# Two transformer blocks in one kernel: norms in two parts, and small work moved beside products

## The chip, the cores and the metric

One core of one Trainium2 chip. The time is that of one execution on the device, in microseconds (us). The kernel runs all its matrix products on TensorE (PE) with float32 data, and each product is three passes over split operands. VectorE (DVE), ScalarE (ACT) and GpSimd (POOL) prepare operands and do everything between the products; SyncE (SP) issues the loads.

## The reference

512 tokens of width 1024 go through two blocks, one after the other.

First block: `h = rms_norm(x, attn_norm)`; `proj = h @ w_in` gives queries, keys and values of a stick-breaking attention of 8 heads (sb), and the latent inputs `cq` (384 columns) and `ckv` (256, with 32 more for a rotary key) of a second attention of 8 heads (MLA) whose heads are normed and rotated by position. `x = x + concat(rms(sb), rms(mla)) @ w_o`. Then a feed-forward by product keys (PEER): `h = rms_norm(x, ffn_norm)`, keys `h @ peer_w_q`, the best 16 of 128 x 128 experts for each of 8 heads, and `x = x + sum(g * gelu(h . u[idx]) * v[idx])`.

Second block: `mod = silu(c) @ w_ada + b_ada` is cut into `sh1, sc1, g1, sh2, sc2, g2`; `hn = rms(x, norm1_g) * (1 + sc1) + sh1`; a mixer of three parts (6 Fox heads with a running sum of log gates, 4 mLSTM heads, 6 MoBA heads); `x = x + g1 * (y @ w_out)`; `hn = rms(x, norm2_g) * (1 + sc2) + sh2`; `x = x + g2 * ((silu(hn @ w_gate) * (hn @ w_up)) @ w_down)`.

## The kernel before, in words

The order of the work is written out by hand, engine by engine; nothing reorders it. Tokens lie in 4 tiles of 128 on the partitions, and the normed input of a product lies transposed as 8 chunks of 128 features by 512 tokens. Every float32 operand is kept as a high and a low part (`hhi`/`hlo`, `whi`/`wlo`), and a product of one chunk is three matmuls (L329 to L331). Weights come through one stream: a load of up to 128 x 1024, a cast to the high part on ScalarE (L198), and a subtraction for the low part (L200) on VectorE, or on GpSimd where the entry says so; two blocks are prepared ahead.

Two shapes of product: `tok_gen` (tokens on the output's partitions, weights streaming, four banks, one for each token tile) and `feat_gen` (features on the partitions, 512 tokens streaming, one bank). `beside` runs a second generator of small steps in step with a product, one step after each group of three matmuls; `mix` does so with a budget of time.

The norms (`Norm`, L382) take the token tiles in a given order. Three tiles have their sums early, the last one late, since the product before ends with it. `late` scales three tiles, transposes them for four chunks (L423), scales the last tile when its own reciprocal root is there (L431), then goes on chunk by chunk: transpose the last tile into the same bank (L436), and `norm_out` over all 512 columns (L444). With a shift, `norm_out` is a scaled and shifted copy, a cast, and a subtraction; without, a scaled cast and one fused subtraction. The product that follows starts after that.

Where the small work stands: the trigonometric tables of the rotary embedding come after the products `cq` and `ckv` on VectorE (L670 to L705), ahead of the roots that norm these (`latent_T`). The heads of MLA are normed and rotated beside products (`head_norm_gen`, L736), then transposed (`head_T`, L768). The sb queries and keys for head pairs 0 to 3 are products of `feat_gen`; pairs 0, 1 and 2 stand beside the head norms, pair 3 beside the first attention (L857). The PEER expert tiles `u` (128 experts each, 384 of the 512 tokens) are made in three places: 40 early ones during the scores and the building of the gate matrix, the rest in the big loop over 128 key rows. The Fox queries and keys are normed beside the next product (`fox_q`, `fox_k`, L1440 to L1460), and the side generator goes on at once from the norm to its transposes (L1421). The modulation (`ada_gen`) runs on GpSimd, one block after each weight block that is fetched. The rows `g1`, `g2` are spread over all partitions by eight small products with a diagonal matrix (`row_from_cols`, L1332), each by itself, ahead of what needs them.

```python
def beside(main, side):
    for ns in main:
        yield ns
        r = next(side, None)
```

## Time and profile before

| | us |
|---|---|
| median of 3 runs | 2392.91 (2389.0 to 2395.34) |
| the profiled execution's own time | 2386.05 |
| its span | 2384.3 |
| TensorE busy | 2272.4 (95%) |
| VectorE busy | 1603.8 (67%) |
| GpSimd busy | 1085.2 (46%) |
| ScalarE busy | 967.2 (41%) |
| mean granted TensorE clock | 0.971 of 2.4 GHz |

The busy time of TensorE counts a matmul at either clock level; the slices of the page with a granted clock of 8 tenths are those in which part of the time ran at 1.2 GHz. Idle time of the other engines costs nothing by itself.

### The profile page before, as it was taken

The page shows a single profiled execution, that of the slowest core. Times are in us where ns is not written, and L with a number is a line of the kernel's source. Part 1 is how long each engine was busy: PE and PEld are TensorE (multiplying, and loading weights), DVE is VectorE, ACT ScalarE, POOL GpSimd, SP SyncE. Part 2 cuts the span into 40 slices and gives each one's busy share as a digit, 9 for nine tenths or more (in the row PEclk, how much of TensorE's full clock was granted, in tenths as well). Part 3 has the DMA queues.
Part 4 walks back from the last instruction along what each step waited for, and adds up shares of the span by engine and source line. Part 5 has one row for each costly group of instructions (what it writes and reads, how often), then busy time and mean ns, then how long its engine had stood idle before and what let it go on. Part 6 is the DMA issues. An engine that isn't in the chain of part 4 may idle for free.

```text
span 2384.3 us, 31909 instructions
## 1 busy us (share of the span) xinstructions
PE 2272.4 (95%) x11721; PEld 1948.5 (82%) x11721; DVE 1603.8 (67%) x2979; ACT 967.2 (41%) x1712; POOL 1085.2 (46%) x763
## 2 busy tenths in 40 slices
PE   7899999988989999999999999999799998999999
PEld 7777778878878888888888888888797776888787
DVE  5666639999967788888888877875675355433322
ACT  4556633446763333333333333335454434222211
POOL 4460024645766666776667666643656102500000
PEclk9998999999999999999999999999899899999999
DMA  5430042325688888998989888962342112423231
GB/s 169 137 115 1 11 154 88 104 96 197 238 292 304 306 303 298 319 313 310 331 306 320 307 307 306 317 235 90 128 131 93 45 36 71 158 92 98 85 112 56
DMA packets 174936, 439.91 MB, mean 184 GB/s; under 512 B 16956, under 2 KB 71100, under 8 KB 171708
## 3 DMA queue, kind: packets, MB, share of 16 engines
q1 hardware_dynamic: 136188, 301.28, 37.6%
q0 software_dynamic: 36864, 134.23, 15.5%
q10 hardware_dynamic: 1728, 2.36, 0.3%
q8 instruction: 92, 1.51, 0.3%
q14 instruction: 64, 0.52, 0.1%
HBM read 406.10 MB, written 31.72 MB: 184 GB/s over the span
## 4 chain that ended last, share of the span: by engine, by line
PE 70%; DVE 15%; issue 5%; POOL 4%; ACT 3%; DMA 2%; SPq 0%; ACTq 0%; POOLq 0%; DVEq 0%
PE bank L331 20%; PE bank L329 20%; PE bank L330 20%; DVE ohAB L1114 3%; DVE ohA L1121 3%; PE bank L571 2%; POOL rows L1241 2%; PE bank L582 2%; POOL wlo L200 2%; PE bank L563 1%; DVE wlo L200 1%; DMA w<-in_uT_dram 1%; PE bank L811 1%; DVE eq L1054 1%; DMA w<-in_peer_v_dram 1%
## 5 line engine op out<-in xcount | busy, mean ns | idle before, releaser
L200 POOL TENSOR_TENSOR wlo<-w,whi 128x1024 fp32r<-128x1024 f32 (+2 forms) x154 | 398.4, 2590 | 416.8 <-ACT whi L198 367.9
L331 PE MATMUL bank<-hhi,wlo 128*128 128x384 f32 (+1 forms) x1600 | 576.0, 360 | 11.3 <-POOL wlo L200 10.9
L329 PE MATMUL bank<-hhi,whi 128*128 128x384 f32 (+1 forms) x1600 | 579.7, 362 | 0.7 <-ACT ge L914 0.7
L330 PE MATMUL bank<-hlo,whi 128*128 128x384 f32 (+1 forms) x1600 | 573.3, 358 | 1.4 <-DVE hlo L455 1.4
L198 ACT CAST whi<-w 128x1024 fp32r<-128x1024 f32 (+4 forms) x414 | 420.9, 1024 | 322.2 <-PE bank L331 173.8
L200 DVE TENSOR_TENSOR wlo<-w,whi 128x1024 fp32r<-128x1024 f32 (+2 forms) x260 | 326.9, 1259 | 277.3 <-ACT whi L198 275.4
L331 PEld LDWEIGHTS bank<-hhi,wlo 128*128 128x128 f32 x1600 | 303.5, 190 | 39.2 <-POOL wlo L200 16.3
L329 PEld LDWEIGHTS bank<-hhi,whi 128*128 128x128 f32 x1600 | 303.5, 190 | 34.1 <-issue 4.1
L330 PEld LDWEIGHTS bank<-hlo,whi 128*128 128x128 f32 x1600 | 303.4, 190 | 30.2 <-DVE hlo L455 2.0
L330 PE MATMUL bank<-wlo,ch 128*128 128x512 f32 x768 | 304.7, 397 | 4.5 <-DVE wlo L200 4.4
L329 PE MATMUL bank<-whi,ch 128*128 128x512 f32 x768 | 304.3, 396 | 4.3 <-DMA w<-in_uT_dram 2.8
L331 PE MATMUL bank<-whi,cl 128*128 128x512 f32 x768 | 304.4, 396 | 0.0
L1219 DVE TENSOR_TENSOR cl<-ge,ch 128x384 fp32r<-128x384 f32 x125 | 148.5, 1188 | 140.4 <-ACT ch L1218 139.5
L1241 POOL DMA_INDIRECT rows<-in_peer_v_dram,eidx x128 | 183.2, 1432 | 109.7 <-DVE acc L1264 81.8
L1241 POOL DMA_INDIRECT rows<-in_peer_u_dram,eidx x128 | 178.5, 1394 | 99.6 <-DVE junk L1259 75.3
L1259 DVE SCALAR_TENSOR_TENSOR junk<-rows,h 128x1024 bf16<-128x1024 f32 x128 | 188.3, 1471 | 0.5 <-DMA rows<-in_peer_u_dram,eidx 0.2
L1264 DVE SCALAR_TENSOR_TENSOR acc<-rows,coefg,acc 128x1024 f32<-128x1024 f32 x127 | 181.6, 1430 | 0.7 <-DMA rows<-in_peer_v_dram,eidx 0.4
L330 PEld LDWEIGHTS bank<-wlo,ch 128*128 128x128 f32 x768 | 144.8, 189 | 36.6 <-DVE wlo L200 5.3
L329 PEld LDWEIGHTS bank<-whi,ch 128*128 128x128 f32 x768 | 144.8, 188 | 36.2 <-ACT ch L1212 3.1
L331 PEld LDWEIGHTS bank<-whi,cl 128*128 128x128 f32 x768 | 144.9, 189 | 35.7 <-DVE cl L1219 0.6
L329 PE MATMUL bank<-whi,hhi 128*128 128x384 f32 (+3 forms) x448 | 170.5, 381 | 0.0
L914 ACT ACTIVATE ge<-bank 128x384 f32<-128x384 f32 x116 | 57.1, 493 | 269.8 <-PE bank L331 265.7
(384 smaller groups left out, 3553.5 us busy)
## 6 DMA issues: line engine op xcount, KB each, us to landing
w<-in_uT_dram SPq DMA_DIRECT2D x128, 512.0 KB
w<-in_peer_v_dram SPq DMA_DIRECT2D x128, 512.0 KB
ada_w<-in_w_ada_dram SPq DMA_DIRECT2D x96, 256.0 KB
gdram<-gs SPq DMA_DIRECT2D x24, 1024.0 KB
gblk<-gdram SPq DMA_DIRECT2D x16, 1536.0 KB
w<-in_w_gu_dram SPq DMA_DIRECT2D x44, 512.0 KB
w<-in_w_down_dram SPq DMA_DIRECT2D x22, 512.0 KB
w<-in_w_pq_dram SPq DMA_DIRECT2D x16, 512.0 KB
```

Of the source, the lines that this page charges most:

```text
L198: nc.scalar.copy(hi[:, :n], t[:, :n])
L200: (eng or nc.vector).tensor_tensor(lo[:, :n], t[:, :n], hi[:, :n].bitcast(F32), op=OP.subtract)
L329: nc.tensor.matmul(o, ah, bh, start=start, stop=False)
L330: nc.tensor.matmul(o, ah, bl, start=False, stop=False)
L331: nc.tensor.matmul(o, al, bh, start=False, stop=stop)
L914: nc.scalar.activation(t, b[:, :DTOK], AF.Gelu)
L1114: nc.vector.tensor_tensor(AB.rearrange("p c b i t -> p (c b) i t"), iota4, IJ[:, n].rearrange("p c (b t) -> p (c b) t", t=2).unsqueeze(2) ...
L1121: nc.vector.tensor_tensor(A[:, c], AB[:, 0], g_, op=OP.mult)
L1219: nc.vector.tensor_sub(cl, t, ch.bitcast(F32))
L1241: nc.gpsimd.indirect_dma_start(out=r, out_offset=None, in_=A["peer_" + kind], in_offset=bass.IndirectOffsetOnAxis(ap=eidx[:, k:k + 1], axi ...
L1259: nc.vector.scalar_tensor_tensor(junk, r, 1.0, h2, op0=OP.mult, op1=OP.mult, accum_out=preg[:, k:k + 1])
L1264: nc.vector.scalar_tensor_tensor(acc, r, coefg[:, k:k + 1], acc, op0=OP.mult, op1=OP.add)
```

## The change

Nine edits, all of order and grouping; what is computed is the same.

1. `Norm` no longer keeps banks for all four tiles. `late` transposes three tiles of all eight chunks and writes their 384 columns at once; the last tile is scaled after chunk 3 and is transposed and written by a generator `tail` in two halves of four chunks, at given steps of the product that follows (`with_tail`).
2. `tok_gen` has `head`: the first two weight blocks are taken tile by tile, the last tile last. It is used for `cq` and for `fvg`.
3. The tables go into a generator that runs beside `cq`.
4. The ffn norm is followed by two `u` tiles ahead of the keys' product (`HEAD`); one more `u` tile is early (`SPILL` 13, `EARLY` 41).
5. The sb products of pair 1 (queries) and pair 3 (queries) go ahead of the transposes of the MLA heads; 16 products with the tables become 4.
6. Norm 1 of the second block takes its tiles as 3, 2, 1, 0; the pools of the mixer open ahead of `late`.
7. `fox_q`, `fox_k` and `moba_heads` yield six more steps (`SLACK`) between norm and transposes; `ada_gen` multiplies with `tensor_scalar`.
8. `feat_pair` (first gate and up pair) runs over 384 columns and then over 128. The modulation beside the gated product starts after this pair and ends before the last but one.
9. The rows `g1`, `g2` are made by `row_gen`, a step at a time beside `out` block 0 and beside the last two gate products.

```diff
-NPRE = 4
+SLACK = 6
+TAIL = (4, 7)
+HEAD = 2
-U0 = 8
+U0 = 10
-SPILL = tuple(LEAD + 4 + 8 * k for k in range(12))
+SPILL = tuple(LEAD + 4 + 7 * k for k in range(13))
...
         def late(self, g):
...
-            for c in range(NPRE):
-                first(c)
-            W.ahead(2)
-            drain(g)
-            x, t, r = self._to(3)
...
+            def last():
+                drain(g)
+                x, t, r = self._to(3)
+                nc.vector.tensor_scalar(t[0], x[0], r, None, op0=OP.mult)
+                nc.scalar.mul(t[1], x[1], r)
+            for c in range(KC):
                 b = bank()
                 for i in range(3):
                     tt = self.order[i]
+                    nc.tensor.transpose(b[:, tt * P:(tt + 1) * P], self.chunk(i, c), ident)
+                sh = None if self.shift is None else self.shift[:, c:c + 1]
+                norm_out(b[:, cols], hhi[:, c, cols], hlo[:, c, cols], self.scale[:, c:c + 1], sh, self.temp, c % 2)
+                if c == 1:
+                    W.ahead(2)
+                if c == 3:
+                    last()
+                if c == 5:
+                    W.ahead(3)
+            self.tail = self.tail_gen()
+        def tail_gen(self):
+            tt = self.order[3]
+            cols = slice(tt * P, (tt + 1) * P)
+            for c0 in (0, 4):
+                b = bank()
+                for k in range(4):
+                    c = c0 + k
+                    nc.tensor.transpose(b[:, k * P:(k + 1) * P], self.chunk(3, c), ident)
+                if self.shift is None:
+                    for k in range(4):
+                        c = c0 + k
+                        norm_out(b[:, k * P:(k + 1) * P], hhi[:, c, cols], hlo[:, c, cols], self.scale[:, c:c + 1],
+                                 None, None)
+                else:
...
+                    t4 = t.rearrange("p (k n) -> p k n", k=4)
+                    nc.scalar.copy(hhi[:, c0:c0 + 4, cols], t4)
+                    nc.vector.tensor_sub(hlo[:, c0:c0 + 4, cols], t4, hhi[:, c0:c0 + 4, cols].bitcast(F32))
+                yield
...
+        if head:
+            ws = [(cp, W.get((key, cp), LOOK - n)) for n, cp in enumerate(cps[:2])]
+            b.extend(bank() for _ in range(NT))
+            for tt in head:
+                for cp, w in ws:
+                    yield from block(cp, w, tt)
...
-        for c in range(kc):
-            w_ = slice(c * P, (c + 1) * P)
-            for (wh, wl), b in zip(ws, bs):
-                mm3(b, (wh[:, w_], wl[:, w_]), (hi[:, c, :], lo[:, c, :]), c == 0, c == kc - 1)
-                yield 3 * S / 2.4
+        for t_ in (slice(0, 3 * P), slice(3 * P, S)):
+            for c in range(kc):
+                w_ = slice(c * P, (c + 1) * P)
+                for (wh, wl), b in zip(ws, bs):
+                    mm3(b[:, t_], (wh[:, w_], wl[:, w_]), (hi[:, c, t_], lo[:, c, t_]), c == 0, c == kc - 1)
+                    yield 3 * (t_.stop - t_.start) / 2.4
...
+    def with_tail(main, nx, at):
+        for k, ns in enumerate(main):
+            yield ns
+            if k + 1 in at:
+                next(nx.tail, None)
...
-                nc.gpsimd.tensor_tensor(w, w, col_, op=OP.mult)
+                nc.gpsimd.tensor_scalar(w, w, col_, None, op0=OP.mult)
...
-    proj_tok("cq", hhi, hlo, KC, 384, lambda tt, b: nc.scalar.copy(cqk[:, tt, :384], b[:, :384]))
+    drain(beside(with_tail(tok_gen("cq", hhi, hlo, KC, 384, lambda tt, b: nc.scalar.copy(cqk[:, tt, :384], b[:, :384]),
+                                   head=range(NT)), nx, TAIL), tables()))
...
         for k, x0 in enumerate((64, 80, 80, 64)):
-            for tt in range(NT):
-                nc.vector.tensor_mul(tabs[k][:, tt], s4[:, tt, :, x0:x0 + 16],
-                                     tr[:, tt, k, :][:, None, :].to_broadcast([P, NH, 16]))
-            yield 800.0
+            nc.vector.tensor_mul(tabs[k], s4[:, :, :, x0:x0 + 16],
+                                 tr[:, :, k, :].unsqueeze(2).to_broadcast([P, NT, NH, 16]))
+            yield 700.0
...
     mix(sbqk_gen(0), fill)
+    mix(sbqk_gen(1, (0,)), fill)
     fill.finish()
...
-    mix(sbqk_gen(1), fill, 0.9)
+    mix(sbqk_gen(1, (1,)), fill, 0.9)
     mix(sbqk_gen(2), fill, 0.9)
+    mix(sbqk_gen(3, (0,)), fill, 0.9)
     fill.finish()
...
+        nx = Norm(lambda tt: xs[:, tt, :], (0, 1, 2, 3), g_ffn, None, o1)
         drain(tok_gen(("o", 1), hhi, hlo, KC, 512, norm_behind(nx, o_evac(1)), O_ORDER, nx.order))
         nx.late(nx.rest)
+        for n in range(HEAD):
+            drain(with_tail(u_gen(), nx, ((6,), (2,))[n]))
...
-        nx = Norm(lambda tt: xs[:, tt, :], (3, 0, 1, 2), n1, sh1, None)
+        nx = Norm(lambda tt: xs[:, tt, :], (3, 2, 1, 0), n1, sh1, None)
...
+        nx.half = lambda: wk.tile([P, S], F32, name="nT_h", tag="f512", bufs=FB2)
+        nx.late(nx.rest)
         y = b2.tile([P, NT, D], F32, name="y")
...
-        proj_tok("fvg", hhi, hlo, KC, 398, ev_fv)
+        drain(with_tail(tok_gen("fvg", hhi, hlo, KC, 398, ev_fv, head=nx.order), nx, TAIL))
...
         def fox_q():
             yield from tq.norm()
+            for _ in range(SLACK):
+                yield
...
-            yield
+                yield
+            for _ in range(SLACK - 3):
+                yield
             yield from fox_T(tk.t, fkg, kTf)
...
-        late_["pool"], late_["g1r"] = b3, row_from_cols(g1c, b3, "g1r")
-        drain(out0)
+        late_["pool"], late_["g1r"] = b3, b3.tile([P, D], F32, name="g1r")
+        drain(beside(out0, row_gen(g1c, b3, late_["g1r"])))
...
             if f == 0:
-                drain(feat_pair((("gate", f), ("up", f)), hhi, hlo, KC, (ev_gate, ev_up)))
+                drain(with_tail(feat_pair((("gate", f), ("up", f)), hhi, hlo, KC, (ev_gate, ev_up)), nx, (8, 11)))
+                ada = ada_gen(tl, range(10, 12))
+                W.tick = ada_tick
             else:
-                proj_feat(("gate", f), hhi, hlo, KC, ev_gate)
+                if f == NF - 2:
+                    drain(ada)
+                    W.tick = None
+                    row = row_gen(g2c, b4, g2r)
+                drain(beside(feat_gen(("gate", f), hhi, hlo, KC, ev_gate), row))
```

`row_gen` makes the same eight diagonal matrices and products as `row_from_cols`, one for each step, the product of a matrix one step after the matrix.

## Rows read from the trace of the kernel before

**Rows 1.** Part 1 of the page: busy time, share of the span, instructions.

```profile
PE 2272.4 (95%) x11721; PEld 1948.5 (82%) x11721; DVE 1603.8 (67%) x2979; ACT 967.2 (41%) x1712; POOL 1085.2 (46%) x763
```

**Rows 2.** What TensorE waited for: total us, times, longest us.

```profile
PE bank L423 <- DVE rs_u L338: 21.9, 4, 11.8
PE bank L331 <- POOL wlo L200: 10.9, 9, 2.5
PE bank L1421 <- DVE cum L1449: 7.9, 1, 7.9
PE bank L375 <- DVE cqk L369: 6.8, 2, 6.3
PE bank L436 <- DVE nT_x L431: 5.8, 3, 2.1
PE bank L1421 <- DVE fx_t L1456: 4.4, 1, 4.4
PE bank L1339 <- DVE dg L1338: 4.3, 3, 2.4
PE bank L768 <- DVE m_q L760: 3.5, 1, 3.5
PE bank L436 <- DVE xb L431: 3.2, 1, 3.2
PE bank L768 <- DVE m_k L760: 1.6, 1, 1.6
```

**Rows 3.** Windows: length; busy us (count) PE, PEld, DVE, ACT, POOL; PEclk; DMA; GB/s.

```profile
21.80:38.90 17.10, 17.10 (x100) 17.10 (x99) 6.67 (x9) 6.92 (x12) 12.54 (x10) 1.00 0.44 138
70.65:75.80 5.15, 5.15 (x19) 4.36 (x20) 1.68 (x3) 1.50 (x3) 4.21 (x4) 0.51 0.29 94
222.40:239.60 17.20, 17.20 (x65) 11.95 (x63) 12.93 (x36) 10.30 (x24) 0.00 (x0) 0.50 0.00 1
327.80:340.50 12.70, 7.19 (x33) 6.49 (x33) 10.48 (x32) 6.99 (x10) 2.36 (x1) 0.65 0.34 116
510.00:690.00 180.00, 161.45 (x1346) 150.07 (x1346) 173.38 (x173) 120.72 (x280) 114.91 (x89) 0.95 0.58 205
715.00:1616.00 901.00, 894.29 (x4340) 786.43 (x4340) 724.88 (x771) 311.14 (x433) 579.84 (x339) 1.00 0.87 304
1682.50:1693.60 11.10, 3.22 (x12) 3.08 (x13) 7.82 (x12) 1.16 (x2) 8.56 (x6) 0.54 0.38 120
1712.40:1721.00 8.60, 4.21 (x20) 4.06 (x20) 4.46 (x7) 1.71 (x3) 6.53 (x6) 0.80 0.52 160
1885.00:1912.00 27.00, 25.89 (x87) 19.29 (x88) 9.45 (x31) 12.98 (x28) 5.77 (x13) 0.50 0.00 1
1947.80:1953.80 6.00, 4.25 (x18) 3.33 (x17) 3.40 (x10) 1.27 (x3) 0.00 (x0) 0.72 0.00 0
2249.80:2256.80 7.00, 4.49 (x18) 3.55 (x18) 3.43 (x10) 1.39 (x3) 0.00 (x0) 0.76 0.05 20
```

**Rows 4.** Timeline of VectorE, 52 to 71 us: start, us, instruction.

```profile
52.05 0.48 DVE L670 MEMSET chmask<- 128x512 f32 x1
...
60.18 0.22 DVE L705 TENSOR_TENSOR trig<-ang,r_k_rope_g 128x64 f32<-128x64 f32 x1
...
70.09 0.74 DVE L369 TENSOR_SCALAR cqk<-cqk,lt 128x384 f32<-128x384 f32 x2
```

**Rows 5.** Timeline of TensorE at 357.7 us: sixteen matmuls of 128 columns.

```profile
357.74 1.95 PE L993 MATMUL bank<-psc,pq 128*128 128x128 f32 x16
```

**Rows 6.** Timeline of VectorE in the last norm.

```profile
1993.28 2.20 DVE L347 TENSOR_TENSOR rs_t<-rs_t,nr_r 128x1 f32<-128x1 f32 x1
...
1995.51 0.16 DVE L349 SCALAR_TENSOR_TENSOR nr_r<-rs_t,nr_r 128x1 f32<-128x1 f32 x1
...
1998.85 0.69 DVE L455 TENSOR_TENSOR hlo<-nT_s,hhi 128x512 fp32r<-128x512 f32 x1 [0.69 <-ACT hhi L454]
...
2002.28 0.69 DVE L455 TENSOR_TENSOR hlo<-nT_s,hhi 128x512 fp32r<-128x512 f32 x1 [0.69 <-ACT hhi L454]
```

More of the change, by code (lines that the diff above doesn't have):

```diff
@@ L434, in late @@
-            for c in range(KC):
-                b = self.banks[c]
-                nc.tensor.transpose(b[:, tt * P:(tt + 1) * P], t[:, c * P:(c + 1) * P], ident)
-                sh = None if self.shift is None else self.shift[:, c:c + 1]
-                norm_out(b, hhi[:, c, :], hlo[:, c, :], self.scale[:, c:c + 1], sh, self.work, c % 2)
-                if c == 4:
-                    W.ahead(3)
-                if c + NPRE < KC:
-                    first(c + NPRE)
+                    nc.tensor.transpose(b[:, tt * P:(tt + 1) * P], self.chunk(i, c), ident)
@@ L687, in build @@
[L687 to L706 removed]
+    trig = []
@@ L1328, in build, with row_gen @@
     pst.close()
-    def row_from_cols(cols, pool, name):
-        t = pool.tile([P, D], F32, name=name)
-        for hh in range(2):
-            b = bank()
-            for k in range(4):
-                dg = pool.tile([P, P], F32, name="dg", bufs=2)
-                nc.vector.tensor_scalar(dg, ident, cols[:, hh * 4 + k:hh * 4 + k + 1], None, op0=OP.mult)
-                nc.tensor.matmul(b[:, k * P:(k + 1) * P], ones, dg, start=True, stop=True)
-            nc.scalar.copy(t[:, hh * 512:(hh + 1) * 512], b)
-        return t
-    with tc.tile_pool(name="nrm", bufs=1) as nrm:
-        nx.work = nrm
-        nx.late(nx.rest)
+    def row_gen(cols, pool, t):
+        b = dg = None
+        for k in range(9):
+            if k and k % 4 == 0:
+                nc.tensor.matmul(b[:, 384:512], ones, dg, start=True, stop=True)
+                nc.scalar.copy(t[:, (k - 4) * P:k * P], b)
+            elif k:
+                nc.tensor.matmul(b[:, (k - 1) % 4 * P:(k - 1) % 4 * P + P], ones, dg, start=True, stop=True)
+            if k == 8:
+                return
+            if k % 4 == 0:
+                b = bank()
+            dg = pool.tile([P, P], F32, name="dg", bufs=2)
+            nc.vector.tensor_scalar(dg, ident, cols[:, k:k + 1], None, op0=OP.mult)
+            yield
     with ExitStack() as st:
@@ L1462, in moba_heads @@
             yield from heads.norm()
+            for _ in range(SLACK):
+                yield
             yield from moba_T(heads.t, gain, dst)
```

216 lines of the change are left out of this document (129 added, 87 removed).

## The prediction

> **What bounds the kernel now.** The first part of the page gives TensorE 2272.4 us of work in a span of 2384.3, 95%; no other engine is above 67% [rows 1]. So a microsecond is won only where TensorE idles, where it runs at its lower clock, or where VectorE holds it for a whole stage. The view of what TensorE waited for names the idle places, and most of the large ones are one wait each [rows 2]: 11.8 us at the start and some 10.1 more over three later norms (first tiles' roots), 7.9 and 4.4 at the Fox heads, 6.3 for the normed latent, 3.5 and 1.6 for the MLA heads, 4.3 over the diagonal matrices, 3.2 and 5.8 for the norms' last tiles. The windows say what the stages are like [rows 3]: the big loop (715 to 1616) has TensorE busy 894.29 of 901.00, so work taken out there is won in full; from 510 to 690 VectorE is busy 173.38 of 180.00 and TensorE 161.45, so there VectorE sets the pace. The last thing to read in the windows is the granted clock. Behind each large wait it is about half: 0.51 from 70.65 to 75.80 behind the 6.3 us, 0.54 around the 7.9. It is also half in two attention stretches (222.4 to 239.6, 1885 to 1912) where TensorE hardly idles [rows 3]. These levels are 1.2 and 2.4 GHz, and work at the lower one takes about twice as long.
>
> **Prices used.** A matmul over 384 columns: 17.10 us over 100 = 0.171 [rows 3]; so 0.228 for 512, by the ratio. One of 128 columns: 1.95 us over 16 = 0.12 [rows 5].
>
> **Part 1, tables beside cq: -8.3.** On VectorE the tables run from 52.05 to 60.4 (8.35 us), and the step that TensorE waits for, the scaled latent, comes at 70.09 [rows 4]. All of what lies between (squares, roots) starts behind them. 8.35 earlier, that step lies ahead of the end of the values' product (the wait of 6.3 us ends at 70.65), and some 0.5 of the 6.3 us is left. With the wait goes the lower clock behind it: 5.15 us at 0.51 is about 2.5 lost. Sum -5.8 - 2.5. The cover: in cq VectorE is busy 6.67 of 17.10 [rows 3], so 8.35 fit; without that cover the tables would delay hlo and cost up to what they save. Bounds -5 (the clock stays low) and -9.
>
> **Part 2, the first norm split: -2.** The 3.2 us wait for the last tile [rows 2] goes; its eight transposes (1.0) stay, now inside cq, and I leave 0.8 for the last tile coming late behind the tables. 3.2 - 0.4 - 0.8 = 2. Bounds 0 and -4.
>
> **Part 3, MLA heads: -6.5.** Waits of 3.5 and 1.6 [rows 2]. Ahead of each now stands one more sb product, 24 matmuls x 0.228 = 5.5 us, longer than either wait. These are not new work; one leaves the first attention, where TensorE is busy in all of the window that I read. Low clock behind the 3.5, in proportion to part 1 (2.5 x 3.5 / 6.3), 1.4. The sum -3.5 - 1.6 - 1.4. That 16 small VectorE products become 4 is not in it: it only shortens a chain that is then hidden. Bounds -4 (waits for hlo of heads move) and -8.
>
> **Part 4, the ffn norm and two u tiles: +2.** Between 327.8 and 340.5 TensorE is busy 7.19 of 12.70 at clock 0.65 [rows 3]. A u tile needs the first three token tiles only: 24 x 0.171 = 4.1 us. Two of them now stand ahead of the keys' product: I put their start at 336.3 (the 24 first transposes at the low clock), so that product starts at 336.3 + 8.2 + 1.0 (tail) + 1.4 (low clock) = 347, 6.5 later than now. All that hangs on its scores is VectorE's (510 to 690), so the shift passes through. In return the big loop has one tile less: -4.1, in full. One tile less beside the gate matrix is worth only -0.5, since VectorE bounds there. +6.5 - 4.1 - 0.5 = +2. The ends: nothing is won back, +6; the shift is 1.5 only and the stretch gives 1 back, -3.
>
> **Parts 5 and 8, the two norms with a shift: +3 and -0.5.** Of `norm_out` with a shift, two chunks of 512 columns are 3.43 us apart on VectorE (1998.85 to 2002.28, rows 6). Bound for 384 columns: 3.43 x 0.75 = 2.57 and 3.43; I take 2.75, nearer the ratio. Eight chunks take 11.0, and the last tile's instructions stand behind the eighth in VectorE's order. Norm 1: the product's head has 12 groups (3 x 2 x 2) of 3 x 0.18 = 6.5 us before it needs the last tile, which comes some 2 us after the eighth chunk; TensorE waits there for about as long as it saved (one wait of the 5.8 over three), and the modulation may now start earlier, on GpSimd, during the norm: +3, between -2 and +6. Norm 2: the pair's 48 matmuls of 512 (10.9) become 48 x 0.171 + 48 x 0.12 = 14.0, +3.1, and the tail costs 1.0; against it go a wait of 2.1 for the last tile and the longest wait for a low part on GpSimd, 2.5 [rows 2], since the modulation starts after the pair: -0.5, between -4 and +4.
>
> **Part 7, the Fox heads: -12.** TensorE waits 7.9 and 4.4 [rows 2]; it has 3.22 busy at 0.54 in one window and 4.21 at 0.80 in the other, some 1.6 and 1.0 lost to the clock [rows 3]. Six steps more are 6 x 3 x 0.171 = 3.1 us later that it asks: 4.8 and 1.3 of the waits are left if VectorE's chain ends when it does now. It need not. A tiny operation that takes 0.16 takes 2.20 in another norm [rows 6], and GpSimd is busy 8.56 of the 11.10 us of the stall with the modulation [rows 3]. In the changed kernel the modulation can start earlier (the pools open before the norm, its loads with them), so less of it should be piled up here. I take half of the 6.1 as left: -9.2 - 2.6 = -12. Ends: only the shift, -6; all gone, -15.
>
> The Trainium skill ("SBUF — State Buffer", Who interferes with whom) says that a VectorE instruction with two SBUF inputs contends with a GpSimd instruction that reads SBUF, and that the one that came second waits whole. The 2.20 us agree. By that rule `tensor_scalar` on GpSimd, which still reads SBUF, takes away no block, and only how much of the modulation is left over there would count; this part would be -6 and not -12, which is the rival called port below.
>
> **Part 9, rows of g1 and g2: -3.7 and -4.3.** 1947.8 to 1953.8 and 2249.8 to 2256.8 [rows 3] hold the eight diagonal products by themselves; their 16 matmuls (two passes each) at 0.12 stay: 6.0 - 1.9 and 7.0 - 1.9, less 0.4 and 0.8 of other work in those windows. VectorE's share is hidden by the products. The ends: -2 and -4.5 for the first, -3 and -5 for the second.
>
> Sum: -8.3 - 2 - 6.5 + 2 + 3 - 0.5 - 12 - 3.7 - 4.3 = -32.3. On the profiled execution's 2386.05 this is 2353.8; the median of the runs shown lies 6.9 above that execution, so the forecast for the median is 2392.9 - 32.3 = 2361. With the parts' ends taken as independent the sum holds about 15 either way: 2346 to 2376.
>
> **The rivals.**
> *Port.* VectorE's chains stay as long as now, since GpSimd's low parts and modulation lie beside them: the Fox part gives only the -6 of its shift, norm 1 costs +6, norm 2 +4. That is +6 + 3 + 4.5 = 13.5 less won: 2374. For it speak the 2.20 us of rows 6; against it that the waits of parts 1, 3 and 9 don't hang on GpSimd.
> *Everything hidden.* The tails come in time and the modulation is out of the way: norm 1 -2, norm 2 -4, Fox -15, ffn -3: 16.5 more: 2345. VectorE's 11.0 for eight chunks speaks against it.
> *No gain: the clock.* Slower than before by one mechanism: TensorE's lower clock in the attentions. 17.2 and 27.0 us already run at half there with TensorE busy 17.20 and 25.89 [rows 3], and one dense product of 5.5 us is taken out of the first. If the lower level spreads over the stages around them, each microsecond of it costs half. To cost the 32 it needs 64 us more of the lower level; at 80 us the time is 2401. For it speaks that nothing in those two rows but the kind of work tells them from other stretches; against, that the change takes long waits away, behind which the clock falls, and leaves the attentions' own instructions as they are.
>
> **How the numbers follow.** Forecast 0.56, port 0.20, everything hidden 0.10, the clock at its full price 0.06, and 0.08 for the clock at half of it with the port (within 0.3%, about 7 us, the least that a measurement of this kernel can tell from no change). Faster 0.86, same 0.08, slower 0.06. The range goes from 2340, just beyond everything hidden, to 2384, which leaves out the two cases of no gain.
>
> **What would show it.** The wait for the latent (L369) gone or under 1 us, and full clock behind it. No wait at L768. The waits at L1421 together about 3 us; still 6 would be the port. The keys' product starting near 347. In norm 1, a wait of TensorE for hlo inside the head of fvg of about 2. The pair over gate and up 14 us long. No L1339 stretch by itself. The two windows of attention at half clock much as they are; any longer stretch of half clock there, and the prediction is wrong for the third reason.

## The result, and the profile after

The changed kernel takes 2358.15 us (median of 4 runs, 2351.38 to 2358.26); the kernel before, on the same chip, 2390.95 (2386.07 to 2395.34). The ratio is 0.9856 [0.9829, 0.9883]: faster, by 32.8 us between the medians and by 27.8 between the two profiled executions (2386.05 and 2358.26). Some executions run at a lower mean clock and take over 1.5% longer; medians and ratios leave them out. The sum of the steps was -32.3. That agrees better than its terms do, and in part by luck: parts 1, 2, 5, 8 and 9 fell short by 12.9 us together, and 8.5 came from parts 3, 4 and 7 and from stages for which nothing was forecast.

The first part of the page (busy time, share of the span, instructions), to be read beside [rows 1]:

```profile
PE 2261.8 (96%) x11769; PEld 1944.4 (83%) x11769; DVE 1586.2 (67%) x2983; ACT 971.3 (41%) x1744; POOL 1120.7 (48%) x763
```

What TensorE waited for, to be read beside [rows 2] (total us, times, longest us):

```profile
PE bank L449 <- DVE rs_u L343: 18.6, 3, 11.6
PE bank L336 <- POOL wlo L203: 10.2, 11, 2.2
...
PE bank L1435 <- DVE dg L1441: 4.3, 2, 2.5
PE bank L380 <- DVE mlo L374: 3.8, 1, 3.8
...
PE bank L334 <- ACT hhi L486: 3.4, 2, 2.7
...
PE bank L380 <- DVE cqk L374: 2.9, 2, 1.5
...
PE bank L335 <- DVE hlo L501: 1.6, 2, 1.5
PE bank L468 <- DVE nT_h L443: 1.3, 1, 1.3
```

The waits of the head transposes are gone: no line names L851 (MLA, L768 before) or L1520 (Fox, L1421 before). The waits for the diagonal matrices (`dg`) kept their 4.3 us, and the norms' last tiles are waited for under new names (`hhi` L486, `nT_h` L443).

Cut at the same products on TensorE, the two profiled executions compare by stage like this (us; each time is of one execution):

```
                                               before   after   change  forecast
start to end of the latents' two products       85.75   79.38    -6.4    -10.3  (parts 1, 2)
  of it: to the end of cq                       38.88   38.79
MLA heads, first sb products                   124.36  117.20    -7.2     -6.5  (part 3)
sb attention                                    68.35   66.43    -1.9      0
ffn norm to the PEER scores                     26.80   32.77    +6.0     +6.5  (part 4)
scores and gate matrix                         332.65  332.07    -0.6     -0.5  (part 4)
big loop, to norm 1                            937.37  930.93    -6.4     -4.1  (part 4)
norm 1 to the end of fvg                        25.89   29.69    +3.8     +3    (part 5)
end of fvg to the first Fox score               71.59   58.79   -12.8    -12    (part 7)
Fox attention                                   73.97   70.39    -3.6      0
MoBA and mLSTM                                 147.44  148.80    +1.4      0
out product with the row g1, to norm 2          44.82   42.51    -2.3     -3.7  (part 9)
norm 2 and the first pair                       22.98   27.50    +4.5     +2.0  (part 8 without its -2.5)
gated product with the row g2                  241.78  239.29    -2.5     -6.8  (part 9, and the -2.5 of part 8)
```

Part 8 counts on a wait of 2.5 for a low part that goes away. In the kernel before, that wait stands in the gated product and not in norm 2 or the pair, which end at 2014.45; so its -2.5 belongs to the last row:

```profile
2023.09 0.50 PE L331 MATMUL bank<-hhi,wlo 128*128 128x512 f32 x1 [2.52 <-POOL wlo L200]
```

The windows of the changed kernel for the main ones (length; busy us and count of PE, PEld, DVE, ACT, POOL; granted clock; DMA share; GB/s):

```profile
38.79:79.38 40.59, 37.71 (x214) 32.55 (x213) 20.00 (x41) 20.00 (x45) 28.74 (x20) 1.00 0.43 139
79.38:196.58 117.20, 117.20 (x676) 100.18 (x674) 76.43 (x202) 72.43 (x172) 60.90 (x36) 1.00 0.34 113
...
1611.24:1640.93 29.69, 24.90 (x127) 23.05 (x128) 18.33 (x38) 16.36 (x29) 14.18 (x10) 0.89 0.37 114
1640.93:1699.72 58.79, 58.79 (x367) 58.18 (x367) 30.07 (x68) 30.58 (x54) 38.07 (x26) 1.00 0.40 130
1699.72:1770.11 70.39, 68.62 (x442) 62.14 (x442) 44.18 (x142) 41.08 (x102) 56.59 (x38) 1.00 0.40 132
1770.11:1918.91 148.80, 144.32 (x665) 106.83 (x664) 70.19 (x204) 59.65 (x136) 45.30 (x51) 0.89 0.18 57
...
1961.42:1988.92 27.50, 23.43 (x129) 21.46 (x129) 15.39 (x33) 14.57 (x25) 4.74 (x2) 0.83 0.11 39
1988.92:1993.52 4.60, 4.60 (x12) 3.63 (x13) 2.42 (x3) 2.70 (x4) 1.94 (x1) 0.50 0.00 0
```

In the second and fourth of these TensorE is busy for the whole window at full clock: nothing is left to win there but work. And between the end of `fvg` and the first Fox score VectorE is busy 30.07 us for 68 instructions; the kernel before needed 40.24 for 66 (first row below). Its work became shorter, which no step of the forecast had priced.

The Fox attention is 3.6 us shorter for a plain reason: the steps move products ahead of the first score. There are 442 matmuls in it, 460 before; 18 x 0.171 = 3.1 us, and the stretch ahead of it has that much more. So the two stages are read together from here on: 145.56 before, 129.18 after, -16.4.

### The profile page after: what moved, and what is told of

The parts are those of the page before. It is cut to its first block, busy times and chain, and to the rows that moved or that the text cites. A ratio compares the mean times of both kernels' runs of the same rounds, so it can differ in the third digit from the quotient of the medians.

```text
span 2356.6 us, 32050 instructions
## 1 busy us (share of the span) xinstructions
PE 2261.8 (96%) x11769; PEld 1944.4 (83%) x11769; DVE 1586.2 (67%) x2983; ACT 971.3 (41%) x1744; POOL 1120.7 (48%) x763
## 4 chain that ended last, share of the span: by engine, by line
PE 74%; DVE 12%; ACT 4%; DMA 4%; issue 3%; POOL 2%; SPq 0%; ACTq 0%; POOLq 0%; DVEq 0%
PE bank L334 22%; PE bank L336 22%; PE bank L335 21%; DVE ohAB L1209 3%; DVE ohA L1216 3%; PE bank L632 2%; PE bank L643 2%; DMA w<-in_uT_dram 1%; DMA w<-in_peer_v_dram 1%; PE bank L624 1%; POOL wlo L203 1%; ACT whi L201 1%; POOL rows L1336 1%; DVE wlo L203 1%; PE bank L896 1%
## 5 line engine op out<-in xcount | busy, mean ns | idle before, releaser
L336 PE MATMUL bank<-hhi,wlo 128*128 128x384 f32 (+2 forms) x1616 | 581.6, 360 | 10.3 <-POOL wlo L203 10.2
L334 PE MATMUL bank<-hhi,whi 128*128 128x384 f32 (+2 forms) x1616 | 587.6, 364 | 2.4 <-ACT hhi L492 0.9
L335 PE MATMUL bank<-hlo,whi 128*128 128x384 f32 (+2 forms) x1616 | 579.9, 359 | 2.4 <-DVE hlo L501 1.6
L336 PEld LDWEIGHTS bank<-hhi,wlo 128*128 128x128 f32 x1616 | 308.9, 191 | 38.6 <-POOL wlo L203 14.7
L334 PEld LDWEIGHTS bank<-hhi,whi 128*128 128x128 f32 x1616 | 309.4, 191 | 34.6 <-issue 4.1
L335 PEld LDWEIGHTS bank<-hlo,whi 128*128 128x128 f32 x1616 | 309.3, 191 | 30.0 <-DVE hlo L501 2.2
L1336 POOL DMA_INDIRECT rows<-in_peer_u_dram,eidx x128 | 175.1, 1368 | 78.9 <-DVE junk L1354 57.3
L705 POOL TENSOR_SCALAR ada_w<-ada_w,c_c 128x512 f32<-128x512 f32 x84 | 149.9, 1784 | 100.1 <-DMA ada_w<-in_w_ada_dram 99.6
```

What stands on the lines that cost most here:

```text
L334: nc.tensor.matmul(o, ah, bh, start=start, stop=False)
L335: nc.tensor.matmul(o, ah, bl, start=False, stop=False)
L336: nc.tensor.matmul(o, al, bh, start=False, stop=stop)
L705: nc.gpsimd.tensor_scalar(w, w, col_, None, op0=OP.mult)
L1336: nc.gpsimd.indirect_dma_start(out=r, out_offset=None, in_=A["peer_" + kind], in_offset=bass.IndirectOffsetOnAxis(ap=eidx[:, k:k + 1], axi ...
```

## The experiments

The attention stages run for a varying share of their time at the lower clock with the same instructions: MoBA and mLSTM take 147.2 to 156.7 us in the fourteen profiled executions, and over 156 in those of experiments 1, 6, 7 and of the first kernel of 10. So medians scatter by some us, and verdicts rest on stages, one profiled execution of each kernel. A ratio is against runs of the kernel before on the same chip. Where no attention lies in them these repeat: the stretch from `fvg` to the first Fox score is 58.78 to 58.80 us in the profiled executions of eight kernels.

**1. The steps in front of the Fox transposes taken out.** Not all of them go: the change also moved a step of `fox_k` into its loop over the four token tiles, and the three steps more that this gives ahead of the keys' transposes stay with `SLACK = 0`.

```diff
-SLACK = 6
+SLACK = 0
```

> The changed kernel with SLACK = 0: no extra steps between the norm of the Fox (and MoBA) heads and their transposes; all else as changed. Theory (the modulation, which now starts earlier, no longer lies beside VectorE's chain, so the chain itself became short, and the six steps only add the last bit): the two waits at the Fox transposes come back as 1 to 2 us each, almost no lower clock behind them, the whole is 2 to 6 us slower than the changed kernel (2360 to 2364). Rival (the six steps did it, the chain is as long as before): waits of 4 us and more each come back, with half clock behind them, 9 to 14 us slower (2367 to 2372).

Median 2361.15, ratio 0.9884 [0.9858, 0.991]. From `fvg` to the first Fox score 57.27 us, with TensorE busy in all of it: the waits at the Fox heads, 12.3 us before, don't come back, though most of the steps, the visible part of part 7, are gone. (The 1.5 us less are 9 matmuls that now come behind the score.) But the Fox attention took 78.91 us at a granted clock of 0.91, 70.39 at 1.00 with the steps; both together 136.18 for 129.18. This profiled execution, with 2371.97 us, is the slowest of five; the others took 2359.56 to 2361.42, so the 7.0 is not what the steps are worth as a rule. Experiment 10 takes that up.

**2. The multiplication of the modulation in its old form.**

```diff
-col_ = csil[:, c:c + 1]
+col_ = csil[:, c:c + 1].to_broadcast([P, 512])
-nc.gpsimd.tensor_scalar(w, w, col_, None, op0=OP.mult)
+nc.gpsimd.tensor_tensor(w, w, col_, op=OP.mult)
```

> The changed kernel with the modulation multiplied on GpSimd as before, by tensor_tensor with a broadcast column in place of tensor_scalar. Theory (GpSimd's modulation is off the path that sets the end): the multiplications get shorter (1.30 us on average in the kernel before against 1.57 in the changed one), GpSimd is busy some 20 to 30 us less, and the time stays within 3 us of the changed kernel. Rival (port: what GpSimd reads holds up VectorE): the time moves by more than 5 us with it.

Median 2367.75, ratio 0.9925 [0.9897, 0.9954]: about half of the gain is gone, for an edit that I had priced at nothing. The MLA heads take 123.91 us again (117.20 with the new form) and the two Fox stages 132.07 (129.18); waits of 3.5 for `m_k` (L851) and 2.3 for `fx_t` (L1520) are back.

**3. Old form and `SLACK = 0`; and the new form alone, in the kernel before.** Two kernels: the edits of 1 and 2 together, and the kernel before with nothing changed but

```diff
-col_ = csil[:, c:c + 1].to_broadcast([P, 512])
+col_ = csil[:, c:c + 1]
-nc.gpsimd.tensor_tensor(w, w, col_, op=OP.mult)
+nc.gpsimd.tensor_scalar(w, w, col_, None, op0=OP.mult)
```

> The changed kernel with both: the modulation multiplied by tensor_tensor again and no extra steps (SLACK = 0). Measured by the stretch from the end of fvg to the first Fox score: 71.9 us before, 58.8 changed, 57.3 without the steps, 61.3 with tensor_tensor. Theory (a tensor_tensor on GpSimd holds up VectorE's norm chain, a tensor_scalar does not, or less; the steps are only a cover against that): both Fox waits come back, 2 to 6 us each, and the stretch is 65 to 70. Rival (the modulation's earlier start alone took the waits away): 62 or less.

> The kernel before with one edit of the change alone: the modulation multiplied on GpSimd by tensor_scalar in place of tensor_tensor with a broadcast column (96 instructions). My prediction priced this at nothing. Theory (it holds up VectorE less wherever VectorE's chain sets the end): the waits at the Fox transposes (7.9 and 4.4) and at the MLA heads (3.5 and 1.6) shrink, the stretch from the end of fvg to the first Fox score falls from 71.9 to 60 to 67, the whole is 5 to 15 us faster than before. Rival (the form makes no difference by itself, its longer 1.57 us against 1.30 even costs): within 3 us of before.

Medians 2373.85 (0.9942 [0.9918, 0.9966]) and 2372.82 (0.9935 [0.9904, 0.9967]). Here are the windows from `fvg` to the first Fox score, of the kernel before, of the kernel before with the new form, and of the changed kernel with the old form, with `SLACK = 0` and with all steps (columns as above):

```profile
1653.65:1725.24 71.59, 59.32 (x348) 57.67 (x348) 40.24 (x66) 29.52 (x50) 46.05 (x35) 0.90 0.46 151
```

```profile
1642.38:1704.73 62.35, 58.02 (x349) 56.77 (x348) 31.55 (x66) 29.24 (x51) 49.56 (x31) 0.95 0.51 164
```

```profile
1651.55:1720.05 68.50, 61.56 (x358) 60.16 (x357) 36.42 (x67) 30.46 (x52) 33.97 (x28) 0.93 0.39 125
```

```profile
1646.85:1708.15 61.30, 58.98 (x367) 58.11 (x367) 36.37 (x68) 30.58 (x54) 33.45 (x28) 1.00 0.41 129
```

One edit on GpSimd takes 8.7 us from VectorE's busy time (40.24 to 31.55, both 66 instructions), and of the 12.3 us of waits at the Fox heads 4.3 are left. With the Fox attention behind it, so that moved products don't count, the two stages take:

```
                          before's order       new order, SLACK = 0   new order, all steps
old form on GpSimd                145.56                   142.26               132.07
new form on GpSimd                137.89                   136.18               129.18
```

The new order, which starts the modulation earlier (GpSimd is busy 33.97 us of the stretch instead of 46.05) and keeps three steps at the keys, is worth 3.3 with the old form; the new form by itself 7.7; the other steps 10.2 with the old form and 7.0 with the new one, the form 2.9 once all steps are there. They share a part of their gain, since form and steps cure the same waits; the 7.0 is clock in the attention and no wait (experiment 1).

Where VectorE's time went is seen in the groups of its instructions. The multiplication of a Fox head's norm, 128 x 384 with both inputs in SBUF, in the same order of kernels, and then in the changed kernel (line, engine, operation, count | busy us, mean ns | idle before):

```profile
L1388 DVE TENSOR_TENSOR fx_t<-fx_t,rs_r 128x384 f32<-128x384 f32 x16 | 18.6, 1216 | 0.1
```

```profile
L1388 DVE TENSOR_TENSOR fx_t<-fx_t,rs_r 128x384 f32<-128x384 f32 x16 | 10.8, 727 | 0.1
```

```profile
L1487 DVE TENSOR_TENSOR fx_t<-fx_t,rs_r 128x384 f32<-128x384 f32 x16 | 19.9, 1294 | 0.1
```

```profile
L1487 DVE TENSOR_TENSOR fx_t<-fx_t,rs_r 128x384 f32<-128x384 f32 x16 | 19.0, 1235 | 0.1
```

```profile
L1487 DVE TENSOR_TENSOR fx_t<-fx_t,rs_r 128x384 f32<-128x384 f32 x16 | 10.9, 735 | 0.1
```

With the old form it takes 1.22 to 1.29 us, with the new one 0.73 here and 0.67 to 0.79 in all eleven kernels that have it, whatever else is changed. And the price is GpSimd's, in its own groups, before and after:

```profile
L644 POOL TENSOR_TENSOR ada_w<-ada_w,c_c 128x512 f32<-128x512 f32 x84 | 109.3, 1301 | 125.8 <-DMA ada_w<-in_w_ada_dram 125.5
```

```profile
L705 POOL TENSOR_SCALAR ada_w<-ada_w,c_c 128x512 f32<-128x512 f32 x84 | 149.9, 1784 | 100.1 <-DMA ada_w<-in_w_ada_dram 99.6
```

GpSimd has the time: in the kernel before with the new form it idles 12.8 us of the window shown above. The timelines show both sides. Before, GpSimd's operations stand back to back, and four multiplications of VectorE take 4.94 us (start, us, instruction):

```profile
1682.45 1.03 POOL L644 TENSOR_TENSOR ada_w<-ada_w,c_c 128x512 f32<-128x512 f32 x1
1683.56 1.68 POOL L645 TENSOR_TENSOR ada_a<-ada_a,ada_w 128x512 f32<-128x512 f32 x1
1685.20 1.35 POOL L644 TENSOR_TENSOR ada_w<-ada_w,c_c 128x512 f32<-128x512 f32 x1
1686.62 1.46 POOL L645 TENSOR_TENSOR ada_a<-ada_a,ada_w 128x512 f32<-128x512 f32 x1
...
1683.56 4.94 DVE L1388 TENSOR_TENSOR fx_t<-fx_t,rs_r 128x384 f32<-128x384 f32 x4
```

After, the same four take 3.50, beside GpSimd's two operations; and a multiplication on GpSimd can itself be held, to 4.16 us at 142.49:

```profile
1664.90 3.50 DVE L1487 TENSOR_TENSOR fx_t<-fx_t,rs_r 128x384 f32<-128x384 f32 x4
...
1664.79 1.57 POOL L705 TENSOR_SCALAR ada_w<-ada_w,c_c 128x512 f32<-128x512 f32 x1 [5.52 <-DMA ada_w<-in_w_ada_dram]
1666.44 1.53 POOL L706 TENSOR_TENSOR ada_a<-ada_a,ada_w 128x512 f32<-128x512 f32 x1
...
142.49 4.16 POOL L705 TENSOR_SCALAR ada_w<-ada_w,c_c 128x512 f32<-128x512 f32 x1 [5.94 <-DMA ada_w<-in_w_ada_dram]
```

Taken one by one, these four show which instruction of GpSimd holds VectorE. The second starts while `tensor_scalar` runs and is not held; the fourth starts while the addition runs, which is `tensor_tensor` in both forms, and takes three times as long:

```profile
1665.81 0.55 DVE L1487 TENSOR_TENSOR fx_t<-fx_t,rs_r 128x384 f32<-128x384 f32 x1
...
1666.74 1.65 DVE L1487 TENSOR_TENSOR fx_t<-fx_t,rs_r 128x384 f32<-128x384 f32 x1
```

Of the sixteen such multiplications in the changed kernel two take 1.65 us, both beside an addition, and the others at most 0.99. In the kernel before eleven take 1.39 to 1.66, beside additions and multiplications alike.

The Trainium skill ("SBUF — State Buffer", Who interferes with whom) makes VectorE's two-input instruction contend with a GpSimd instruction that reads SBUF; both forms read it, and 727 ns against 1216 differ. The measurement decides. The addition has no broadcast operand and holds VectorE all the same, so the hold does not need the broadcast; why `tensor_scalar` does not hold it is not shown.

In part 3 the form is one of two things needed: the old form with the sb products moved leaves 123.91, the new one with the old order 122.54 (a wait of 3.4 at L768), both together 117.20.

**4. Both norms with a shift in one piece again.** The two norms transpose four chunks, take the last tile into the same banks and write all 512 columns, as before; the pair over 512.

```diff
+nx.whole = True                     # norm 1, norm 2
-drain(with_tail(tok_gen("fvg", ..., head=nx.order), nx, TAIL))
+proj_tok("fvg", hhi, hlo, KC, 398, ev_fv)
-for t_ in (slice(0, 3 * P), slice(3 * P, S)):
+for t_ in (slice(0, S),):
```

> The changed kernel with both norms that have a shift (second block) made whole again: four chunks transposed, the last tile joined into the same bank, 512 columns written at once, products over all 512 columns; the modulation stays where the change put it. Theory (splitting costs there what the two traces differ by: 3.8 us up to the end of the gates' product fvg, 4.8 up to the end of the first gate and up pair): 6 to 9 us faster than the changed kernel (2349 to 2352). My prediction's own terms (+3 and, with a wait of 2.5 gone by the moved modulation, -0.5): 0 to 3 faster. Rival (the loss is GpSimd's modulation moved into norm 1, and clock): no faster, within 2 us.

Median 2352.86, ratio 0.9869 [0.9841, 0.9897]. Norm 1 to the end of `fvg` 26.34 (29.69), norm 2 and its pair 23.17 (27.50), and the product behind it 237.13 (239.29): the split of parts 5 and 8 costs 3.4 and 4.3 us. Of the 4.3, and of the 2.2 behind it, 2.2 each are the clock (part 8 below). Where the time goes in norm 1 stands on VectorE's timeline of the changed kernel:

```profile
1616.72 1.91 DVE L501 TENSOR_TENSOR hlo<-nT_h,hhi 128x384 fp32r<-128x384 f32 x2 [0.58 <-ACT hhi L500]
...
1619.89 0.49 DVE L443 TENSOR_SCALAR nT_h<-xs,nr_r 128x512 f32<-128x512 f32 x1
...
1624.39 1.86 DVE L501 TENSOR_TENSOR hlo<-nT_h,hhi 128x384 fp32r<-128x384 f32 x2 [0.58 <-ACT hhi L500]
```

The last tile's scaling (L443) stands behind the first chunks in VectorE's order, and TensorE, whose order is as fixed, stops twice: for the scaled tile and for the tail's high part.

```profile
1620.53 0.63 PE L468 MATMUL bank<-ident,nT_h 128*128 128x128 f32 x4 [1.32 <-DVE nT_h L443]
...
1628.71 0.70 PE L334 MATMUL bank<-whi,hhi 128*128 128x398 f32 x1 [2.73 <-ACT hhi L486]
```

**5. The subtraction two chunks behind.** Is it the round trip from VectorE over ScalarE and back inside one chunk?

```diff
+pend.append((c, t))
+while len(pend) > (2 if c < KC - 1 else 0):
+    c_, t_ = pend.pop(0)
+    nc.vector.tensor_sub(hlo[:, c_, cols], t_, hhi[:, c_, cols].bitcast(F32))
```

> The changed kernel with the norms that have a shift laid out so that VectorE never stands behind ScalarE's cast: the subtraction for the low part of two chunks is issued behind the scaling of the next. Theory (what the split norms cost is VectorE's order: 2.8 us for two chunks, of which 1.1 are waits for ScalarE's cast): about 1.9 us for two chunks, the last tile ready 3 us earlier; from the first transpose to the end of fvg 24.5 to 26.5 us (29.7 changed, 25.9 before, 26.3 made whole), from the first transpose of norm 2 to the second gate 22 to 25 (27.5, 23.0, 23.2); 5 to 9 us faster in all. Rival (the subtractions are held up by GpSimd's low parts and line up anyway): less than 2 us in each.

Median 2364.15, ratio 0.9883 [0.9845, 0.9921]. Norm 1 28.36 (29.69; at most 26.5 expected), norm 2 23.66 (27.50). In norm 2 that is 3.8 of 4.5, of which 2.2 may be the clock (part 8 below); in norm 1 only 1.3 of 3.8. The rest goes with the split (experiment 4); whether the order on VectorE or the additional instructions cost it was not separated.

**6. The first diagonal matrix six steps earlier than its product.**

```diff
-yield
+for _ in range(1 if k else 6):
+    yield
```

> The changed kernel, with five more steps of the product let by between the first diagonal matrix and its product in row_gen, for both rows. Theory (the first diagonal matrix stands behind a weight's low part on VectorE and TensorE, asked one step later, waits for it: 1.85 and 2.45 us): both waits go, 3 to 6 us faster than the changed kernel (2352 to 2355). Rival (another wait takes their place, since the low part itself is then what TensorE waits for): within 1.5 us.

Median 2360.3, ratio 0.9874 [0.9843, 0.9904]. The waits for `dg` go from 4.3 to 1.1; the stage with g1 takes 41.50 instead of 42.51, the gated product 235.66 instead of 239.29. Of the last 3.6, 2.2 are clock: the first 4.6 us of that product run at 0.50 in the changed kernel (last window above), and not here nor in experiment 4, where it takes 237.13 with the wait still there. So 2.5 of part 9's missing us stood here, 1.0 and 1.5: a matrix of 0.3 us behind a weight's low part of 1.23 on VectorE, with TensorE behind the matrix (changed kernel):

```profile
1921.74 1.23 DVE L203 TENSOR_TENSOR wlo<-w,whi 128x1024 fp32r<-128x1024 f32 x1 [0.25 <-ACT whi L201]
1922.88 0.48 DVE L1441 TENSOR_SCALAR dg<-ident,modc 128x128 f32<-128x128 f32 x2
...
1923.38 0.46 PE L1435 MATMUL bank<-dg,ones 128*128 128x128 f32 x2 [1.84 <-DVE dg L1441]
```

The median is nevertheless 2.2 above the changed kernel's. MoBA and mLSTM took 156.51 in its profiled execution, at a granted clock of 0.82 where the changed kernel had 0.89 in the windows above and the kernel before 0.87; no instruction there is changed (the kernel before, then this one):

```profile
1799.21:1946.65 147.44, 145.47 (x664) 107.62 (x664) 70.90 (x204) 59.91 (x136) 39.87 (x49) 0.87 0.18 58
```

```profile
1774.14:1930.65 156.51, 154.37 (x664) 113.48 (x664) 69.07 (x203) 59.53 (x134) 43.53 (x50) 0.82 0.18 55
```

**7. No u tiles ahead of the keys' product.**

```diff
-HEAD = 2
-U0 = 10
-SPILL = tuple(LEAD + 4 + 7 * k for k in range(13))
+HEAD = 0
+U0 = 8
+SPILL = tuple(LEAD + 4 + 8 * k for k in range(12))
+drain(nx.tail)
```

> The changed kernel without the two expert tiles ahead of the keys' product (HEAD = 0, 12 spilled tiles, 40 early): the ffn norm's last tile then joins at once. Measured from the first transpose of that norm to the end of the gate matrix (364.8 us changed, 359.4 before), and from there to the first transpose of norm 1 (930.9 and 937.4). Prediction's step (two tiles shift all that hangs on the scores by their 8.3 us less the filled idle time, and the big loop has one tile less): first stretch 359 to 362, second 935 to 938, the sum within 3 us of the changed kernel. Rival (the tiles fill idle time for nothing): first stretch as changed or longer, the sum 4 us or more longer.

Median 2364.43, ratio 0.9896 [0.9854, 0.9938]. The scores come 3.3 us earlier (29.46 for 32.77; 362.07 for 364.84 to the end of the gate matrix), and the big loop, with one tile more, takes 930.37 against 930.93 and not the 935 to 938 expected: the tile less, put at -4.1 "in full", wins nothing that can be seen.

**8. The tables behind both latent products again.**

```diff
-drain(beside(with_tail(tok_gen("cq", ...), nx, TAIL), tables()))
+drain(with_tail(tok_gen("cq", ...), nx, TAIL))
 proj_tok("ckv", hhi, hlo, KC, 288, ev_ckv)
+drain(tables())
```

> The changed kernel with the trigonometric tables back behind cq and ckv on VectorE; all else as changed. Prediction's step (the tables hold up the latent's norm and TensorE waits 6.3 us for it, with half clock behind): the stretch from the end of cq to the first product with the latent goes from 40.6 to 45 to 47 us (46.9 before), the wait at the latent's transposes is 5 to 6.5 again. Rival (tensor_scalar and the order of the norm have already shortened that chain): below 43.

Median 2359.26, ratio 0.9879 [0.9834, 0.9924]. The wait for the latent is back (6.2, longest 5.7) and that stretch takes 45.17 (40.59); but `cq` ends at 36.32 instead of 38.79. The tables cost 2.5 where they went and save 4.6 where they were: 2.1 net, not 8.3. Even that is the upper end. In the five other profiled executions with the same instructions up to there (experiments 1, 4, 5, 6, 7) the latents' products end at 80.24 to 81.83, here at 81.49.

Most of what the tables cost is one wait that this kernel doesn't have. In the changed kernel a weight's low part stands behind the last of their instructions on VectorE, and TensorE behind it:

```profile
32.83 0.94 DVE L762 SCALAR_TENSOR_TENSOR ang<-angk,ang 128x128 f32<-128x128 f32 x3
33.70 1.62 DVE L203 TENSOR_TENSOR wlo<-w,whi 128x768 fp32r<-128x768 f32 x2
...
34.70 0.44 PE L335 MATMUL bank<-wlo,hhi 128*128 128x384 f32 x1 [2.15 <-DVE wlo L203]
```

**9. What the experiments keep.** All four norms in one piece, no u tiles ahead, `SLACK = 0`, the earlier matrix; the tables beside `cq`, the moved sb products, the new form and the earlier modulation stay.

> What the runs so far pay for, and nothing else: from the changed kernel, tables beside cq, products moved ahead of the MLA heads' transposes, tensor_scalar on GpSimd, the earlier modulation, and the rows beside products with five steps between the first matrix and its product; all four norms whole as before, no expert tiles ahead of the keys' product, no extra steps at the heads. By the stretches measured: fvg 29.7 to 26, Fox 58.8 to 57, norm 2 to the second gate 27.5 to 23, from there to the down product 239 to 236, ffn norm to the scores 32.8 to 27: 12 to 18 us faster than the changed kernel where the clock in the attentions is the same (2340 to 2347 by the median). Rival (the parts cover for each other, as the steps and tensor_scalar did): a wait comes back at the heads or the keys, and it is less than 6 us faster.

Median 2347.61 (2342.91 to 2350.62), ratio 0.984 [0.9812, 0.9868], 10.5 us below the changed kernel's where 12 to 18 were expected. By stages (ffn norm 26.83 for 32.77, norm 1 25.96 for 29.69, norm 2 23.11 for 27.50, gated product 235.64 for 239.29) it is 17.7 us shorter than the changed kernel, and the two Fox stages give 5.4 of that back (134.55 for 129.18), as in experiment 1.

**10. The steps again, on the kept parts.** With all of them, and with those ahead of the Fox transposes alone.

```diff
-SLACK = 0
+SLACK = 6
```

> The version of the kept parts with the six steps put back ahead of the Fox and MoBA transposes. In the profiled executions the two kernels with the new form and without steps ran the Fox attention at a granted clock of 0.91 and 0.93 (78.91 and 77.03 us), the changed kernel with them at 1.00 (70.39). Theory: the steps, which keep 9 more products ahead of the first score and shorten the wait of 1.5 us for the first head's softmax to 0.5, keep the clock there: from fvg to the first Fox score 58.8, Fox attention 70 to 71 at 1.00, together 129 where the kept parts without steps have 134.6; median some 5 us lower, 2342. Rival: the lower level falls on that stage as it falls on the other attentions, whatever the steps do: the two stages take 133 to 136 together, and the median stays at 2345 to 2350.

> The same with the steps ahead of the Fox transposes alone; the MoBA heads, whose transposes lie inside the Fox attention, go on at once. Theory: it is the start of the attention that decides, so this is as the kernel with all steps: 58.8 and 70 to 71 us, full clock. Rival one: the steps of the MoBA heads count too, since a transpose that waits inside the attention is a second gap: a wait at the MoBA transposes (L1530 in the changed kernel) of 0.5 to 2 us and 2 to 5 us more in that stage. Rival two: nothing of this, the level is the execution's: 133 to 136 for the two stages together.

Medians 2340.57 (0.9809 [0.9766, 0.9852]) and 2342.81 (0.981 [0.977, 0.9851]). The two Fox stages take 129.71 and 129.21, against 134.55 with `SLACK = 0`. The Fox attention of experiment 1 and of the kernel with the Fox steps alone:

```profile
1700.02:1778.93 78.91, 76.55 (x452) 68.81 (x451) 46.28 (x143) 43.05 (x105) 59.67 (x39) 0.91 0.38 123
```

```profile
1693.11:1763.53 70.42, 68.65 (x443) 61.99 (x442) 46.28 (x142) 41.10 (x102) 58.69 (x37) 1.00 0.41 131
```

TensorE waits little in either; what differs is the granted clock. The wait for the first head's softmax is 1.5 us with `SLACK = 0` and 0.5 with all steps, and the clock is 0.67 for the first 10 us of experiment 1's window, then 0.81. That the wait is the cause is not shown: the kernel before has one of 1.3 there, and that of experiment 3 with the old form and `SLACK = 0` one of 1.5, and both keep their clock at 1.00. That the steps go with more of the full clock is seen in few executions: 70.4 to 72.6 us at 0.97 to 1.00 in all nine profiled ones with them, 77.0 and 78.9 in the two with `SLACK = 0` and the new form. Whether the steps do it is not shown either. The steps of the MoBA heads show no effect (129.71 and 129.21). The medians are 7.0 and 4.8 below that of experiment 9, but the first kernel's executions lie in two groups (2338.68 to 2340.57, and 2351.17 and 2352.14), and the intervals overlap the changed kernel's, 0.9856 [0.9829, 0.9883]: likely better by 11 to 18 us, not settled by the ratios.

## Why the prediction came out, point by point

**Parts 1 and 2**: -6.4 for -10.3. The wait for the latent fell from 6.8 us in all to 2.9, where 0.5 was forecast, and the clock behind it is full, as said. Mis-sized: the cover. The step "so 8.35 fit" counted free time of VectorE, not the order. The forecast feared for `hlo`; what the tables delay is a weight's low part, for 2.15 us (experiment 8), and that ate the 2 of the split (start to end of `cq` 38.88 and 38.79).

**Part 3**: -7.2 for -6.5, right in size, but with half of its cause missing: the moved products hide the chain only because it also became shorter by the form on GpSimd (experiments 2 and 3).

**Part 4**: the shift to the scores was right (+6.0 for +6.5; the keys' product started at 331.76, which with the 15.5 us won by then is the 347 forecast). The step that failed is "in return the big loop has one tile less: -4.1, in full". The loop differs by -6.4 between the two executions, but neither the tile nor another part of the change is shown to do that. The kernel before with the new form alone runs the same loop in 929.45, though no modulation runs in it in either kernel, and experiment 7 has no difference. Over all profiled executions it takes 927.7 to 930.4 us with 90 tiles and 927.3 to 932.7 with 89; the 937.37 of the kernel before stand alone. TensorE idles 9.4 to 12.8 us in it with 90 tiles (17.3 in the kernel before) and 12.7 to 15.4 with 89: the tile was filling, in part at least. Why the kernel before's loop was long stays open, and with it some 6 of the 27.8 us.

**Part 5**: +3.8 for +3, by the mechanism named, VectorE's rate over the eight chunks (two take 2.84 us, from 1620.30 to 1623.14 in the changed kernel; 2.75 were forecast). **Part 8**: its wait of 2.5 was counted in the wrong stage; without it the part forecast +2.0 and cost +4.5. The failed term is the 128 columns at full clock. Their 0.11 us spacing doubles from 1983.2 on, and the granted clock is 0.50 for 5.7 us there and for 4.6 more in the gated product, some 2.2 us lost in each. Three other kernels with the same norm and the same waits in the pair keep the full clock and take 25.27: +2.3, as the rest of the sum has it.

**Part 7**: -16.4 over the two stages for -12, and its reason is only half right. The step that failed is "I take half of the 6.1 as left": nothing is left. The new order with the modulation's earlier start, which was to win that half, is worth 3.3; the form on GpSimd, which the forecast and its rival called port both counted as nothing, is worth 7.7 by itself and brings VectorE's chain home. The shift by the steps was real, but once the form is new no wait is left for it; the 3.6 in the attention behind are the moved products.

**Part 9**: -2.3 for -3.7 at g1; at g2, together with the wait of part 8, -2.5 for -6.8. "VectorE's share is hidden by the products" failed: the waits for the first matrices cost 1.0 and 1.5 (experiment 6). Another 2.2 at g2 are the clock of part 8.

**The clock rival** did not happen: the three attention stages together went from 289.76 to 285.62, and 3.1 of that is the moved products. The first one gained 1.9 and the last lost 1.4. But it is the mechanism by which the profiled execution of experiment 1 lost 7 us in the Fox attention and 8 more in the last one.

Of the tells, the missing wait at L768, the 347 and the wait in `fvg` (2.7, for a high part) came as said. The waits at L1421 are gone where 3 us were forecast, the latent is waited for 2.9 us and not under 1, and the pair takes 22.5 us and not 14: it starts beside the norm, at the pace of VectorE's chunks.

## What to carry to other kernels

Try both forms of an operation on GpSimd that runs beside a chain on VectorE, also where GpSimd has time to spare: a longer instruction there made the stage shorter. Free time of an in-order engine is a cover only if nothing that is waited for stands behind what is put there; ask that of each moved instruction (tables, scaled tile, diagonal matrix). Splitting a norm brought the end of `cq` forward by 2.6 us where nothing else stood beside it (36.32 in experiment 8, 38.88 before), and cost 3.4 and some 2 us in the norms with a shift, where VectorE has more to do for each chunk. That this is the difference was not tested.

## What was not expected of the hardware

GpSimd's `tensor_scalar` by a column takes 1.78 us on average in the changed kernel where `tensor_tensor` with the column broadcast takes 1.17 to 1.30, and yet holds up VectorE less: 0.73 us against 1.22 for a 128 x 384 multiplication. One by one it is 0.55 to 0.99 us beside `tensor_scalar` in the changed kernel, and up to 1.66 beside `tensor_tensor` in the kernel before, with a broadcast operand or without.

The same 664 recorded matmuls of MoBA and mLSTM took 147.44 us at a granted clock of 0.87 in the kernel before, and 156.51 at 0.82 in experiment 6, with TensorE busy for 145.47 and 154.37. What decides how much of these stages runs at the lower level, and why the 10.3 us from the first pair on do, stays open.
